# Work taken off GpSimd at the start, the epsilon in a 65th column, one factor moved to a later copy, 512 keys per score product, and an order worked out with other GpSimd durations

## The chip, the cores and the metric

One core of a Trainium2 chip runs the whole kernel. The metric is the device time of one execution in microseconds (us), lower is better. Five engines work side by side: TensorE (PE; its weight loads are a row of their own, PEld), VectorE (DVE), ScalarE (ACT), GpSimd (POOL) and SyncE (SP), which here only issues DMAs.

## The reference, cut to what matters

Two layers on 512 latent and 256 context tokens of width 1024, each of the form x + gate * mixer(adaLN(x)). In both, a token's input u goes through one large product into q, k, v and z, q and k are normalised per head, and the mixer's output is multiplied by silu(z) and goes through an output product.

```
e = silu(cvec) @ mod_w + mod_b                # shift, scale and gate of a layer
u = rms_norm(x, norm_g) * (1 + scale) + shift
q, k, v, z = split(u @ w_in, 4)
q = rms_norm(q, qn_g);  k = rms_norm(k, kn_g) # over 64 columns, eps 1e-6
# layer 0, differential attention, 16 heads (rope on latent q, k):
p = softmax(q k^T / 8);  o = (p[first] - lam * p[second]) @ v
y = rms_norm(o, subln_g) * (1 - lam_init) * silu(z)
# layer 1, neighbourhood attention, 32 heads: 8 x 16 window plus all context keys
o = softmax([q k_band^T / 8 + bias, q k_ctx^T / 8]) @ [v_band, v_ctx]
y = o * silu(z)
out = y @ w_out                               # then x + gate * out
```

## The kernel before

**Numbers.** Every large product is made in three products of rounded parts: a value is split into hi (a ScalarE copy to the rounded format) and lo (value minus hi, one subtraction), and hi*hi, hi*lo and lo*hi are added up in PSUM. The splits are most of the work of ACT and DVE: tiles `whi`/`wlo` for weights, `uhi`/`ulo` or `ufirst` for inputs, `mhl` for the weights of the first modulation, `wTa`/`wTb` for softmax weights.

**Stages.** Both layers work in 16 groups (two heads each). While a group's attention runs, the projection of the next group (`a_project`, `b_project`, PSUM tile `pj`) is laid between its steps. Ahead of layer 0's first group there is an opening: `mod_first` makes the modulation of layer 0 on PE (tile `pmod`, rows copied to `erow`, result in `mod0a`, `mod0b`), `norm_stats` makes the norm of each third of the tokens (`npart`, `nacc`, `nv`, `nr`, `ns`), `scaled` multiplies the input by it in place (`xin`), `first_u` applies the modulation (`ut`) and splits it (`ufirst`), and group 0 is projected as its inputs arrive. Between the layers lie the output product and the residual (`pjo`, `xres`).

**A projected tile** (`a_tile`, 96 times in layer 0; 80 alike in layer 1): `squares` on ACT (`sqk`), `rstd` sums them on DVE (`ssk`), scales and adds eps on POOL (`ssk` again), raises to -0.5 on POOL (`rsk`); `put_q` and `put_k` on DVE (`qd`, `kk`) then feed transposes on PE (`pq`, `pk`). `gate_z` makes z*(1+tanh) on DVE and, in layer 0, multiplies it on POOL by the sub-norm's gain (`Z`).

**After a group's attention in layer 0** (`a_norm`): PE transposes into `po`, ACT squares with a sum into `ms`, POOL adds eps*l^2 (`l0sq`) and raises to -0.5, DVE makes `y`, PE transposes it (`py`), ACT copies it out (`yT`) and it is stored.

**Layer 1's scores** (`b_scores`): for each of 16 groups, 2 heads and 4 query tiles, 256 band keys and 256 context keys, each a product with the hi and the lo part of q: four PE products of 256 columns.

**Order.** Nothing is issued as written. `Plan` records every instruction, estimates its duration (`estimate`), plays the run with a list scheduler (`order`: of the instructions ready on an engine the one recorded first) and issues them in the order played. Each engine then works through its fixed queue, so an instruction that is slower on the chip than in the play holds up what was placed right behind it. `LAG` and `AT` say at which step of a group things are recorded.

Of the kernel before, what the change touches and what calls it, by code (L numbers as in the profile page):

```python
# [10 lines left out]
F32 = mybir.dt.float32  # L11
# [18 lines left out]
def bc(ap, shape):  # L30
# [3 lines left out]
BUFS = dict(x8=2, wraw=2, whi=11, wlo=11, u=6, wT=4, qT=3, K=2, V=6, Z=5, ss=4, rs=4, nm=4,  # L34
            oT=1, y=1, yT=1, sq=1, t2=1, braw=1, tab=1, tab2=1)

# [5 lines left out]
FILL_A, FILL_B = (0, 1, 2, 3, 5, 7, 9, 11, 13, 15, 16, 17), (2, 4, 6, 8, 10, 11, 12, 13)  # L42
START_DVE = (0,)

# [6 lines left out]
NEXT = ((1, 2), (0, 1, 2), (1, 2), (0, 1, 2))  # L51
U_ACT = ((0, 0), (2, 0))
X_POOL, W_POOL, STAT_POOL = (2, 5, 6, 7, 9, 10, 11), (0, 1, 2, 3), ()
POOL_A, POOL_B = (), ()
# [29 lines left out]
class Op:  # L84
# [9 lines left out]
    def estimate(self, name):  # L94

        out, reads, e = self.writes[0], self.reads, self.engine
        n = math.prod(out.shape[1:])
        psum = any(x.space == PSUM for x in [out] + reads)
        if e == "PE":
            return 2.5 + n * (1 if reads[0].dtype == F32R else 2 if name == "transpose" else 4) / 2.4 if n > 2 else 260  # L100
        if e == "ACT":
            return n / 1.2 + (51 if psum else 93) + 93 * (len(self.writes) - 1 + name.startswith("act") * (len(reads) - 1))
        if e == "DVE":
            if name == "tensor_reduce":
                return math.prod(reads[0].shape[1:]) / 0.96 + 66
            if name in ("tensor_scalar", "tensor_copy", "memset") and not psum:
                return n / 1.92 + 69 + 60 * (len(reads) - 1)
            return n / 0.96 + (129 if len(reads) > 2 else 69)
        if e == "POOL":
            if any(x == ALU.pow for x in self.args):  # L110
                return 300 + 165 * n
            return n * 0.83 + 36 if name == "memset" else n * 2.1 + 150
        return max(56, math.prod(out.shape) / 90)
# [166 lines left out]
class K:  # L280
# [4 lines left out]
    def setup(self, es):  # L285
# [15 lines left out]
        self.mhalf = c.tile([P, 16], F32, name="mhalf")  # L301
        nc.vector.memset(self.mhalf, -0.5)

    def load_vecs(self):
# [128 lines left out]

    def norm_stats(self, x, tag="qd", on_pool=False):

# [4 lines left out]
        for kp in range(1, 4):  # L440
            sq = sb.tile([P, 2, 256], F32, name="sq", tag="pb")
            nc.scalar.activation(sq, x[kp], AF.Square)
            (nc.gpsimd if on_pool else nc.vector).tensor_tensor(part, part, sq, ALU.add)
        nc.vector.tensor_tensor(acc, part[:, 0], part[:, 1], ALU.add)
# [97 lines left out]
    def squares(self, x):  # L542
        sq = self.sb.tile([P, 2, P], F32, name="sqk", tag="sq")
        self.nc.scalar.activation(sq, x, AF.Square)
        return sq

    def rstd(self, sq):

        nc, sb = self.nc, self.sb
        ss = sb.tile([P, 4], F32, name="ssk", tag="ss")  # L550
        nc.vector.tensor_reduce(ss, sq.rearrange("p s (h d) -> p (s h) d", d=64), AX.X, ALU.add)
        nc.gpsimd.tensor_scalar(ss, ss, 1.0 / 64, EPS, ALU.mult, ALU.add)
        rs = sb.tile([P, 4], F32, name="rsk", tag="rs")
        nc.gpsimd.tensor_tensor(rs, ss, self.mhalf[:, 0:4], ALU.pow)
        return rs
# [40 lines left out]

    def gate_z(self, pz, dst, mul=None):
        nc = self.nc
        nc.vector.scalar_tensor_tensor(dst, dst, 1.0, pz, ALU.add, ALU.mult)
        if mul is not None:  # L600
            nc.gpsimd.tensor_tensor(dst, dst, mul, ALU.mult)

# [22 lines left out]
    def a_tables(self):  # L625
# [9 lines left out]
        for t in range(4):  # L635
            nc.vector.tensor_tensor(self.rc[:, t], self.rc[:, t], g[:, :, 0:64], ALU.mult)
            nc.vector.tensor_tensor(self.rs_[:, t], self.rs_[:, t], gs[:, :, 0:64], ALU.mult)
        tab2 = sb.tile([P, 2, P], F32, name="tab2", tag="tab2")
        self.gctx, self.subg = tab2[:, 0].rearrange("p (s d) -> p s d", s=2), tab2[:, 1]
        nc.vector.tensor_scalar(self.gctx[:, 0], g[:, 0, 0:64], 0.125, None, ALU.mult)  # L640
        nc.vector.tensor_copy(self.gctx[:, 1], g[:, 1, 0:64])

        nc.sync.dma_start(self.subg, A["subg"].broadcast_to([P, P]))
        nc.vector.tensor_scalar(self.subg, self.subg, 0.5 * (1.0 - LAM_INIT) * math.sqrt(P), None, ALU.mult)

        lv = sb.tile([P, 4, 64], F32, name="lv", tag="sq")
        nc.sync.dma_start(lv, A["lam"].unsqueeze(0).broadcast_to([P, 4, 64]))
# [13 lines left out]
    def a_tile(self, G, half, j, ps):  # L661
# [16 lines left out]
        nc.vector.tensor_tensor(V[:, 1, j], ps[:, 256:384], V[:, 0, j], ALU.subtract)  # L678
        self.gate_z(ps[:, 384:512], Z[:, j], mul=self.subg)
        qd = sb.tile([P, 2, 2, 64], F32, name="qd", tag="qd")  # L680
# [19 lines left out]
    def a_scores(self, g, G, half, j):  # L700
# [25 lines left out]
        nc.vector.scalar_tensor_tensor(sc, l[:, 0:1], self.nlam, r1, ALU.mult, ALU.mult)  # L726
        nc.gpsimd.tensor_tensor(l0sq[:, j : j + 1], l[:, 0:1], l[:, 0:1], ALU.mult)
        nc.vector.scalar_tensor_tensor(p[:, 0], p[:, 1], sc, p[:, 0], ALU.mult, ALU.add)
# [33 lines left out]
    def a_norm(self, g, G, half, oT, l0sq):  # L762
# [6 lines left out]
        for j in range(2):  # L769
            nc.scalar.activation(y[:, j], po[:, j], AF.Square, accum_out=ms[:, j : j + 1])  # L770
        nc.gpsimd.tensor_scalar(l0sq, l0sq, EPS * P, None, ALU.mult)
        nc.gpsimd.tensor_tensor(ms, ms, l0sq, ALU.add)
# [5 lines left out]
    def a_store(self, g, half, y):  # L778
        nc, sb = self.nc, self.sb
        py = self.pm.tile([P, 256], F32, name="py", tag="m")  # L780
        for j in range(2):
            nc.tensor.transpose(py[:, j * P : j * P + P], y[:, j], self.ident)
        if half < 2 and self.keep(0, g, py, slice(half * 256, half * 256 + 256)):
# [7 lines left out]
    def b_tables(self):  # L791
# [4 lines left out]
        self.gb = sb.tile([P, 2, 64], F32, name="gb", tag="tab2")  # L796
        nc.vector.tensor_scalar(self.gb[:, 0], g[:, 0, 0:64], -0.125, None, ALU.mult)
        nc.vector.tensor_copy(self.gb[:, 1], g[:, 1, 0:64])
        self.mask = sb.tile([P, 3, 256], F32, name="mask", tag="tab")
        nc.sync.dma_start(self.mask, A["mask"])  # L800
        self.pp = []
        for i in range(2):
            t = sb.tile([P, 2, 704], F32, name=f"pp{i}", tag="x8")
            nc.gpsimd.memset(t[:, :, 0:64], 0.0)
            nc.gpsimd.memset(t[:, :, 320:384], 0.0)
            self.pp += [t[:, 0], t[:, 1]]
# [62 lines left out]
    def b_bias(self, g, h):  # L869
# [5 lines left out]
        for geo in range(3):  # L875
            o = 128 - 64 * geo
            nc.vector.tensor_tensor(bm[:, geo], self.mask[:, geo], raw[:, o : o + 256], ALU.subtract)
        nc.gpsimd.memset(bm[:, 3], 0.0)
        self.bm[h] = bm

    def b_scores(self, g, G, h):
# [7 lines left out]
        for n in range(4):  # L889
# [10 lines left out]
            nc.vector.tensor_tensor_reduce(out=S2, in0=S2, in1=bm[:, geo : 4 : 3 - geo], op0=ALU.add, op1=ALU.min,  # L900
                                           scale=1.0, scalar=BIG, accum_out=nm)
            if n in (1, 2):
                p = self.pp[2 * h + n - 1]
                dst = p[:, 64:704].rearrange("p (a b) -> p a b", b=320)[:, :, 0:256]
            else:
# [8 lines left out]
    def b_weights(self, pn, kts):  # L914
# [3 lines left out]
        for kt in kts:  # L918
            ns = {0: (0, 1), 1: (0, 1, 2), 2: (1, 2, 3), 3: (2, 3)}.get(kt, (0, 1, 2, 3))
            pw = self.pm.tile([P, 512], F32, name="pwb", tag="m")  # L920
            for n in ns:
                if kt >= 4:
                    o = (384 if n in (1, 2) else 256) + (kt - 4) * P
                else:
                    o = (kt - (0, 0, 1, 2)[n]) * P
                nc.tensor.transpose(pw[:, n * P : n * P + P], pn[n][:, o : o + P], self.ident)
# [60 lines left out]

    def keep(self, layer, g, py, c):

        if g + 1 < NG:  # L990
            return False
        hi, lo = self.direct[layer]
        self.nc.scalar.copy(hi[:, c], py)
        self.nc.vector.tensor_tensor(lo[:, c], py, hi[:, c], ALU.subtract)
        self.kept += c.stop - c.start
# [83 lines left out]
    def run(self):  # L1079
# [12 lines left out]
        with ExitStack() as es:  # L1092
# [21 lines left out]
            with tc.tile_pool(name="ps0", bufs=3, space=PSUM) as ps0:  # L1114
# [3 lines left out]
                next(first)  # L1118
                r = self.norm_stats(xs[0], "Z", 0 in STAT_POOL)
                if SC0:  # L1120
# [11 lines left out]
                for n in range(4):  # L1132
                    for half in range(3):
                        if n == 0 and half:
                            self.scaled(xs[half], self.norm_stats(xs[half], "Z", half in STAT_POOL), half)
                        if half in NEXT[n]:
# [206 lines left out]
```

## Time and profile before

| | us |
|---|---|
| median of 3 runs | 1797.8 (1797.69 to 1799.71) |
| the profiled execution | 1795.94 |
| its span, first to last instruction | 1794.0 |
| PE busy | 1766.6 (98%) |
| PEld busy | 1506.1 (84%) |
| DVE busy | 1480.4 (83%) |
| ACT busy | 970.6 (54%) |
| POOL busy | 517.8 (29%) |

The profiled execution lasts 1.9 us longer than its span and is 1.9 us under the median. Products overlap on PE: a busy time is the time covered by at least one, so it also covers short stalls between two of them.

### The profile page before, as it was taken

Reading aid. Unit: us, or ns where it says so; the run is one execution under the profiler, and the core shown is the slowest. Engines: PE = TensorE matmul, PEld = TensorE weight load, DVE = VectorE, ACT = ScalarE, POOL = GpSimd, SP = SyncE. Lnnn points to the kernel's source line nnn. Section 1 sums busy time; section 2 is a strip of 40 time slices with the busy share of each in tenths; the row PEclk is TensorE's granted clock in tenths of the full one; section 3 lists DMA queues with packets and bytes.
Section 4 is the critical chain, followed back from the end, with each engine's and each line's share of the span. In section 5 each row is a group of like instructions: output and inputs, shape, how many; then the busy total and the mean of one; then the engine's idle time right before and its main releaser. Section 6 shows DMA issues by size and latency. Waiting matters only on the chain.

```text
span 1794.0 us, 29417 instructions
## 1 busy us (share of the span) xinstructions
PE 1766.6 (98%) x10032; PEld 1506.1 (84%) x10032; DVE 1480.4 (83%) x3493; ACT 970.6 (54%) x2654; POOL 517.8 (29%) x859
## 2 busy tenths in 40 slices
PE   7899999999999999999999999999999999999999
PEld 3688888888888888888888988888888888888887
DVE  5889999889999999989867777778878877787863
ACT  4455555555555555555645545555555555555641
POOL 4544344344444434344200021121112111222100
PEclk9999999999999999999999999999999999999999
DMA  7401222212222222223547411212222222112423
GB/s 286 140 16 57 77 69 63 69 54 69 80 77 80 66 80 75 70 92 100 172 126 241 159 52 63 62 63 67 65 73 73 63 74 74 63 62 74 146 89 105
DMA packets 60773, 160.73 MB, mean 90 GB/s; under 512 B 7376, under 2 KB 22096, under 8 KB 59728
## 3 DMA queue, kind: packets, MB, share of 16 engines
q1 hardware_dynamic: 60624, 158.86, 27.3%
q8 instruction: 79, 1.29, 0.3%
q14 instruction: 70, 0.57, 0.1%
HBM read 144.68 MB, written 14.16 MB: 89 GB/s over the span
## 4 chain that ended last, share of the span: by engine, by line
PE 85%; DVE 7%; ACT 4%; POOL 2%; issue 1%; DMA 1%; SPq 0%; DVEq 0%; ACTq 0%
PE pj L277 46%; PE pjo L277 12%; PE S L277 5%; PE oT L277 4%; PE oTb L277 4%; PE pwb L277 4%; PE Sb L277 3%; ACT pexp L277 2%; PE pq L277 2%; POOL ms L277 2%; PE pw L277 2%; PE pk L277 1%; DVE nm L277 1%; DVE y L277 1%; PE py L277 1%
## 5 line engine op out<-in xcount | busy, mean ns | idle before, releaser
L277 PE MATMUL pj<-whi,ufirst 128*128 128x512 f32 x1536 | 523.9, 401 | 2.4 <-ACT ufirst L277 1.9
L277 PEld LDWEIGHTS pj<-whi,ufirst 128*128 128x128 f32 x1536 | 289.5, 189 | 57.9 <-ACT ufirst L277 2.5
L277 PE MATMUL pj<-wlo,ufirst 128*128 128x512 f32 x768 | 302.9, 394 | 0.0
L277 PE MATMUL pj<-whi,uhi 128*128 128x512 f32 (+1 forms) x768 | 279.3, 364 | 0.0
L277 PE MATMUL pj<-whi,ulo 128*128 128x512 f32 (+1 forms) x768 | 276.5, 360 | 0.0
L277 PE MATMUL pj<-wlo,uhi 128*128 128x512 f32 (+1 forms) x768 | 276.0, 360 | 0.0
L277 ACT CAST whi<-wraw 128x512 fp32r<-128x512 f32 x352 | 208.7, 629 | 97.2 <-PE pjo L277 32.6
L277 DVE TENSOR_TENSOR wlo<-wraw,whi 128x512 fp32r<-128x512 f32 x344 | 230.5, 696 | 31.6 <-ACT whi L277 30.7
L277 ACT ACTIVATE pexp<-S,nm 128x768 f32<-128x768 f32 (+1 forms) x192 | 144.0, 757 | 127.9 <-DVE nm L277 127.8
L277 POOL TENSOR_SCALAR ssk<-ssk 128x4 f32<-128x4 f32 x176 | 35.1, 199 | 610.2 <-DVE ssk L277 608.2
L277 PE MATMUL pjo<-yhl,whi 128*128 128x512 f32 (+1 forms) x768 | 208.0, 357 | 0.0
L277 POOL TENSOR_TENSOR rsk<-ssk,mhalf 128x4 f32<-128x4 f32 x176 | 179.4, 1019 | 14.5
L277 PEld LDWEIGHTS pj<-wlo,ufirst 128*128 128x128 f32 x768 | 145.4, 189 | 26.4
L277 PEld LDWEIGHTS pj<-whi,ulo 128*128 128x128 f32 x768 | 145.1, 189 | 18.9
L277 PEld LDWEIGHTS pj<-wlo,uhi 128*128 128x128 f32 x768 | 145.2, 189 | 16.6
L277 PEld LDWEIGHTS pj<-whi,uhi 128*128 128x128 f32 x768 | 145.2, 189 | 16.2
L277 PEld LDWEIGHTS pjo<-yhl,whi 128*128 128x128 f32 x768 | 134.8, 189 | 18.3
L277 DVE TENSOR_REDUCE nm<-S 128x2 f32<-128x1536 f32 (+1 forms) x96 | 133.9, 1395 | 6.2 <-PE S L277 6.1
L277 PE MATMUL pjo<-yhl,wlo 128*128 128x512 f32 (+1 forms) x384 | 136.7, 356 | 0.0
L277 ACT ACTIVATE sqk<-pj 128x256 f32<-128x256 f32 x176 | 67.5, 384 | 124.3 <-PE pj L277 119.8
L277 PE MATMUL S<-KS,qT 128*128 128x256 f32 (+1 forms) x640 | 132.8, 336 | 0.0
L277 ACT CAST wTb<-pwb 128x512 fp32r<-128x512 f32 (+2 forms) x192 | 87.1, 488 | 70.0 <-PE pwb L277 69.5
(161 smaller groups left out, 3483.6 us busy)
## 6 DMA issues: line engine op xcount, KB each, us to landing
wraw<-wa SPq DMA_DIRECT2D x64, 512.0 KB, 3.5
wraw<-wb SPq DMA_DIRECT2D x64, 512.0 KB, 3.6
modw<-modw SPq DMA_DIRECT2D x48, 512.0 KB, 3.7
wraw<-wo SPq DMA_DIRECT2D x24, 512.0 KB, 3.9
wraw<-wo SPq DMA_DIRECT2D x48, 256.0 KB, 3.2
yraw<-yd SPq DMA_DIRECT2D x14, 512.0 KB, 3.8
braw<-rpb SPq DMA_DIRECT2D x32, 192.0 KB, 2.4
yd<-yT SPq DMA_DIRECT2D x30, 128.0 KB, 1.9
```

Source lines behind the costliest of these rows:

```text
L277: op.f(*op.args, **op.kw)
```

## The change

1. In the opening, no subtraction or product runs on POOL any more: 12 of the 16 `mhl` subtractions (`START_DVE`), 7 of the 12 `xin` products (`X_POOL`) and the 8 `wlo` subtractions of group 0 (`W_POOL`) go to DVE. Four `ut` (half 1, even k) go from DVE to ACT (`U_ACT`). The powers (`nr`) stay on POOL.
2. `squares` writes into one constant tile with 65 columns per head, the last of which holds 64*eps; the sum then has eps in it, and the POOL instruction that scaled and added it goes (176 times). The factor 8 that is left over moves into the tables of gains.
3. The sub-norm's gain is no longer multiplied into `Z` (96 POOL products); it is the scale of the copy from `py` (`yT`, and `keep` for the last group).
4. eps*128 is multiplied in where l^2 is made, so that 48 POOL instructions of `a_norm` go.
5. `b_scores` reads context and band keys with one access pattern: two products of 512 columns in place of four of 256. Keys stand in the order context, band, and `bm` and the padded tiles `pp` follow.
6. `estimate` has other durations for POOL, so the order played is another one.

```diff
-START_DVE = (0,)
+START_DVE = (0, 1, 2, 3)
-U_ACT = ((0, 0), (2, 0))
-X_POOL, W_POOL, STAT_POOL = (2, 5, 6, 7, 9, 10, 11), (0, 1, 2, 3), ()
+U_ACT = ((0, 0), (1, 0), (2, 0))
+X_POOL, W_POOL = (), ()
...
             if any(x == ALU.pow for x in self.args):
-                return 300 + 165 * n
-            return n * 0.83 + 36 if name == "memset" else n * 2.1 + 150
+                return 402 + 153 * n
+            if n <= 4:
+                return 957 if name == "tensor_tensor" and n == 2 else 400 if n == 1 else 210
+            return n * 0.83 + 36 if name == "memset" else n * 2.35 + 110
...
+        self.sq = c.tile([P, 4, 65], F32, name="sqk")
+        nc.vector.memset(self.sq[:, :, 64:65], 64 * EPS)
...
     def squares(self, x):
-        sq = self.sb.tile([P, 2, P], F32, name="sqk", tag="sq")
-        self.nc.scalar.activation(sq, x, AF.Square)
-        return sq
+        self.nc.scalar.activation(self.sq[:, :, 0:64], x.rearrange("p s (h d) -> p s h d", d=64), AF.Square)
+        return self.sq
...
-        nc.vector.tensor_reduce(ss, sq.rearrange("p s (h d) -> p (s h) d", d=64), AX.X, ALU.add)
-        nc.gpsimd.tensor_scalar(ss, ss, 1.0 / 64, EPS, ALU.mult, ALU.add)
+        nc.vector.tensor_reduce(ss, sq, AX.X, ALU.add)
...
-    def gate_z(self, pz, dst, mul=None):
+    def gate_z(self, pz, dst):
-        if mul is not None:
-            nc.gpsimd.tensor_tensor(dst, dst, mul, ALU.mult)
...
-        nc.gpsimd.tensor_tensor(l0sq[:, j : j + 1], l[:, 0:1], l[:, 0:1], ALU.mult)
+        nc.gpsimd.tensor_scalar(l0sq[:, j : j + 1], l[:, 0:1], l[:, 0:1], EPS * P, ALU.mult, ALU.mult)
...
-        nc.gpsimd.tensor_scalar(l0sq, l0sq, EPS * P, None, ALU.mult)
...
-        nc.scalar.copy(yT, py)
+        nc.scalar.activation(yT, py, AF.Copy, scale=self.subg)
...
-            for c, k in ((0, k0), (256, 0)):
-                for i in range(2):
-                    nc.tensor.matmul(S[:, c : c + 256], qT[:, i, h, (n % 2) * P : (n % 2) * P + P],
-                                     KS[:, h, k : k + 256], start=(i == 0), stop=(i == 1))
+            k = KS[:, h, 0:512].rearrange("p (a b) -> p a b", a=2)
+            k = type(k)(k.tensor, k.offset, (k.ap[0], (k0, 2), (1, 256)))
+            for i in range(2):
+                nc.tensor.matmul(S, qT[:, i, h, (n % 2) * P : (n % 2) * P + P], k, start=(i == 0), stop=(i == 1))
```

## Rows read from the trace of the kernel before

**Rows 1.** Windows: stretch, length, busy us of PE, PEld, DVE, ACT, POOL; PEclk, DMA.

```profile
0.00:92.00 92.00, 72.55 (x335) 47.27 (x336) 66.60 (x130) 43.62 (x91) 47.08 (x47) 0.94 0.59 208
...
160.00:860.00 700.00, 696.84 (x3823) 587.76 (x3822) 641.34 (x1532) 395.25 (x1223) 290.60 (x497) 1.00 0.23 74
...
1060.00:1700.00 640.00, 640.00 (x3881) 561.87 (x3881) 514.55 (x1272) 356.51 (x923) 124.07 (x210) 1.00 0.23 72
```

**Rows 2.** Waits of PE over the span: us in total, times, longest us.

```profile
PE pmod L277 <- DMA modw<-modw: 9.0, 1, 9.0
PE pmod L277 <- DVE erow L277: 7.5, 4, 3.2
PE pj L277 <- ACT ufirst L277: 1.9, 2, 1.7
PE py L277 <- DVE y L277: 1.3, 6, 0.4
```

**Rows 3.** Timeline of DVE in the opening: start, us for the run of instructions.

```profile
32.77 2.50 DVE L277 TENSOR_SCALAR ut<-xin,mod0a,mod0b 128x256 f32<-128x256 f32 x2
...
73.44 1.05 DVE L277 TENSOR_SCALAR ut<-xin,mod0a,mod0b 128x256 f32<-128x256 f32 x3
...
76.45 1.29 DVE L277 TENSOR_TENSOR wlo<-wraw,whi 128x512 fp32r<-128x512 f32 x2
```

**Rows 4.** Timeline of POOL in the opening.

```profile
32.08 4.31 POOL L277 TENSOR_TENSOR xin<-xin,ns 128x512 f32<-128x512 f32 x3
```

**Rows 5.** Groups of DVE in the stretch 20:85, shapes apart: count, busy us, mean ns.

```profile
L277 DVE TENSOR_SCALAR ut<-xin,mod0a,mod0b 128x256 f32<-128x256 f32 x16 | 12.0, 793 | 0.1
...
L277 DVE TENSOR_TENSOR xin<-xin,ns 128x512 f32<-128x512 f32 x4 | 5.3, 1346 | 4.3 <-ACT ns L277 4.3
...
L277 DVE TENSOR_TENSOR mhl<-modw,mhl 128x512 fp32r<-128x512 f32 x3 | 4.2, 1404 | 0.0
...
L277 DVE TENSOR_TENSOR nacc<-npart 128x256 f32<-128x256 f32 x2 | 2.8, 1414 | 0.0
```

**Rows 6.** Groups of POOL over the span, shapes apart.

```profile
L277 POOL TENSOR_TENSOR Z<-Z,tab 128x128 f32<-128x128 f32 x96 | 54.5, 568 | 0.2
...
L277 POOL TENSOR_SCALAR ssk<-ssk 128x4 f32<-128x4 f32 x176 | 35.1, 199 | 610.2 <-DVE ssk L277 608.2
...
L277 POOL TENSOR_TENSOR mhl<-modw,mhl 128x512 fp32r<-128x512 f32 x12 | 17.2, 1448 | 18.8 <-ACT mhl L277 18.8
```

**Rows 7.** Windows of the opening, columns as in the first group.

```profile
26.00:30.00 4.00, 4.00 (x14) 2.74 (x14) 2.94 (x5) 1.95 (x4) 1.66 (x1) 0.57 1.03 410
```

**Rows 8.** Timeline of PE in layer 1.

```profile
1199.73 0.39 PE L277 MATMUL pj<-wlo,uhi 128*128 128x512 f32 x1
...
1202.68 0.39 PE L277 MATMUL pj<-whi,ulo 128*128 128x512 f32 x1
...
1203.92 1.68 PE L277 MATMUL Sb<-KSb,qT 128*128 128x256 f32 x12
1205.43 0.40 PE L277 MATMUL pj<-whi,uhi 128*128 128x512 f32 x1
...
1208.18 0.64 PE L277 MATMUL Sb<-KSb,qT 128*128 128x256 f32 x4
1208.66 0.60 PE L277 MATMUL pq<-ident,qd 128*128 128x128 f32 x4
```

**Rows 9.** Waits of PE's weight loads over the span.

```profile
PEld py L277 <- DVE y L277: 13.5, 41, 0.7
...
PEld pq L277 <- DVE qd L277: 6.9, 14, 0.7
```

**Rows 10.** Chain that ended last in the stretch 330:352: start, us, what.

```profile
329.34 0.97 POOL ms L277
...
330.38 0.72 POOL ms L277
...
331.12 0.62 DVE y L277 x2
```

More of the change, by code (lines that the diff above doesn't have):

```diff
@@ L34 @@
 BUFS = dict(x8=2, wraw=2, whi=11, wlo=11, u=6, wT=4, qT=3, K=2, V=6, Z=5, ss=4, rs=4, nm=4,
-            oT=1, y=1, yT=1, sq=1, t2=1, braw=1, tab=1, tab2=1)
+            oT=1, y=1, yT=1, t2=1, braw=1, tab=1, tab2=1)
 LAG = dict(pw=2.5, pv=1.5, po=0.5, py=1.5, qka=2, qkb=3, b1=2, b2=1.5, b3=1, bo=0.5, by=3)
@@ L51 @@
 NEXT = ((1, 2), (0, 1, 2), (1, 2), (0, 1, 2))
-U_ACT = ((0, 0), (2, 0))
-X_POOL, W_POOL, STAT_POOL = (2, 5, 6, 7, 9, 10, 11), (0, 1, 2, 3), ()
+U_ACT = ((0, 0), (1, 0), (2, 0))
+X_POOL, W_POOL = (), ()
+SQ_PE = (False, False, False)
 POOL_A, POOL_B = (), ()
@@ L431, in mod_finish, with norm_stats @@
         return r
-    def norm_stats(self, x, tag="qd", on_pool=False):
+    def norm_stats(self, x, tag="qd", on_pe=False):
         nc, sb = self.nc, self.sb
@@ L442, in norm_stats @@
             nc.scalar.activation(sq, x[kp], AF.Square)
-            (nc.gpsimd if on_pool else nc.vector).tensor_tensor(part, part, sq, ALU.add)
+            nc.vector.tensor_tensor(part, part, sq, ALU.add)
         nc.vector.tensor_tensor(acc, part[:, 0], part[:, 1], ALU.add)
@@ L595, in k_transposed @@
         nc.vector.tensor_tensor(KS[0:64, 1, s], pk[64:128], KS[64:128, 1, s], ALU.subtract)
-    def gate_z(self, pz, dst, mul=None):
-        nc = self.nc
-        nc.vector.scalar_tensor_tensor(dst, dst, 1.0, pz, ALU.add, ALU.mult)
-        if mul is not None:
-            nc.gpsimd.tensor_tensor(dst, dst, mul, ALU.mult)
+    def gate_z(self, pz, dst):
+        self.nc.vector.scalar_tensor_tensor(dst, dst, 1.0, pz, ALU.add, ALU.mult)
     def gained(self, out, x, g):
@@ L635, in a_tables @@
         for t in range(4):
[L636 to L643, printed above, removed]
+            nc.vector.scalar_tensor_tensor(self.rc[:, t], self.rc[:, t], 8.0, g[:, :, 0:64], ALU.mult, ALU.mult)
+            nc.vector.scalar_tensor_tensor(self.rs_[:, t], self.rs_[:, t], 8.0, gs[:, :, 0:64], ALU.mult, ALU.mult)
+        tab2 = sb.tile([P, P], F32, name="tab2", tag="tab2")
+        self.gctx = tab2.rearrange("p (s d) -> p s d", s=2)
+        self.subg = c.tile([P, 1], F32, name="subg")
+        nc.vector.tensor_copy(self.gctx[:, 0], g[:, 0, 0:64])
+        nc.vector.tensor_scalar(self.gctx[:, 1], g[:, 1, 0:64], 8.0, None, ALU.mult)
+        nc.sync.dma_start(self.subg, A["subg"].rearrange("a p -> p a"))
         nc.vector.tensor_scalar(self.subg, self.subg, 0.5 * (1.0 - LAM_INIT) * math.sqrt(P), None, ALU.mult)
-        lv = sb.tile([P, 4, 64], F32, name="lv", tag="sq")
+        lv = sb.tile([P, 4, 64], F32, name="lv", tag="qd")
         nc.sync.dma_start(lv, A["lam"].unsqueeze(0).broadcast_to([P, 4, 64]))
@@ L678, in a_tile @@
         nc.vector.tensor_tensor(V[:, 1, j], ps[:, 256:384], V[:, 0, j], ALU.subtract)
-        self.gate_z(ps[:, 384:512], Z[:, j], mul=self.subg)
+        self.gate_z(ps[:, 384:512], Z[:, j])
         qd = sb.tile([P, 2, 2, 64], F32, name="qd", tag="qd")
@@ L782, in a_store @@
             nc.tensor.transpose(py[:, j * P : j * P + P], y[:, j], self.ident)
-        if half < 2 and self.keep(0, g, py, slice(half * 256, half * 256 + 256)):
+        if half < 2 and self.keep(0, g, py, slice(half * 256, half * 256 + 256), self.subg):
             return
         yT = sb.tile([P, 256], F32, name="yT", tag="yT")
-        nc.scalar.copy(yT, py)
+        nc.scalar.activation(yT, py, AF.Copy, scale=self.subg)
         y = self.yd[0][g // 2, :, g % 2, half] if half < 2 else self.ye[g // 2, :, g % 2, 0]
@@ L796, in b_tables @@
         self.gb = sb.tile([P, 2, 64], F32, name="gb", tag="tab2")
-        nc.vector.tensor_scalar(self.gb[:, 0], g[:, 0, 0:64], -0.125, None, ALU.mult)
-        nc.vector.tensor_copy(self.gb[:, 1], g[:, 1, 0:64])
+        nc.vector.tensor_scalar(self.gb[:, 0], g[:, 0, 0:64], -1.0, None, ALU.mult)
+        nc.vector.tensor_scalar(self.gb[:, 1], g[:, 1, 0:64], 8.0, None, ALU.mult)
         self.mask = sb.tile([P, 3, 256], F32, name="mask", tag="tab")
@@ L802, in b_tables @@
         for i in range(2):
-            t = sb.tile([P, 2, 704], F32, name=f"pp{i}", tag="x8")
-            nc.gpsimd.memset(t[:, :, 0:64], 0.0)
-            nc.gpsimd.memset(t[:, :, 320:384], 0.0)
+            t = sb.tile([P, 2, 640], F32, name=f"pp{i}", tag="x8")
+            nc.gpsimd.memset(t[:, :, 256:320], 0.0)
+            nc.gpsimd.memset(t[:, :, 576:640], 0.0)
             self.pp += [t[:, 0], t[:, 1]]
@@ L876, in b_bias @@
             o = 128 - 64 * geo
-            nc.vector.tensor_tensor(bm[:, geo], self.mask[:, geo], raw[:, o : o + 256], ALU.subtract)
-        nc.gpsimd.memset(bm[:, 3], 0.0)
+            nc.vector.tensor_tensor(bm[:, geo + 1], self.mask[:, geo], raw[:, o : o + 256], ALU.subtract)
+        nc.gpsimd.memset(bm[:, 0], 0.0)
         self.bm[h] = bm
@@ L893, in b_scores @@
             qT = G["q"][1 + n // 2]
-            for c, k in ((0, k0), (256, 0)):
-                for i in range(2):
-                    nc.tensor.matmul(S[:, c : c + 256], qT[:, i, h, (n % 2) * P : (n % 2) * P + P],
-                                     KS[:, h, k : k + 256], start=(i == 0), stop=(i == 1))
+            k = KS[:, h, 0:512].rearrange("p (a b) -> p a b", a=2)
+            k = type(k)(k.tensor, k.offset, (k.ap[0], (k0, 2), (1, 256)))
+            for i in range(2):
+                nc.tensor.matmul(S, qT[:, i, h, (n % 2) * P : (n % 2) * P + P], k, start=(i == 0), stop=(i == 1))
             S2 = S.rearrange("p (a b) -> p a b", a=2)
             nm = sb.tile([P, 1], F32, name="nmb", tag="nm")
-            nc.vector.tensor_tensor_reduce(out=S2, in0=S2, in1=bm[:, geo : 4 : 3 - geo], op0=ALU.add, op1=ALU.min,
+            nc.vector.tensor_tensor_reduce(out=S2, in0=S2, in1=bm[:, 0 : geo + 2 : geo + 1], op0=ALU.add, op1=ALU.min,
                                            scale=1.0, scalar=BIG, accum_out=nm)
@@ L903, in b_scores @@
                 p = self.pp[2 * h + n - 1]
-                dst = p[:, 64:704].rearrange("p (a b) -> p a b", b=320)[:, :, 0:256]
+                dst = p.rearrange("p (a b) -> p a b", b=320)[:, :, 0:256]
             else:
@@ L921, in b_weights @@
             for n in ns:
[L922 to L925, printed above, removed]
+                o = (kt - 4) * P if kt >= 4 else 256 + (kt - (0, 0, 1, 2)[n]) * P
                 nc.tensor.transpose(pw[:, n * P : n * P + P], pn[n][:, o : o + P], self.ident)
@@ L985, in b_store, with keep @@
         nc.sync.dma_start(self.yd[1][g // 2, :, g % 2], yT)
-    def keep(self, layer, g, py, c):
+    def keep(self, layer, g, py, c, gain=None):
         if g + 1 < NG:
@@ L992, in keep @@
         hi, lo = self.direct[layer]
-        self.nc.scalar.copy(hi[:, c], py)
-        self.nc.vector.tensor_tensor(lo[:, c], py, hi[:, c], ALU.subtract)
+        if gain is None:
+            self.nc.scalar.copy(hi[:, c], py)
+            self.nc.vector.tensor_tensor(lo[:, c], py, hi[:, c], ALU.subtract)
+        else:
+            self.nc.scalar.activation(hi[:, c], py, AF.Copy, scale=gain)
+            self.nc.vector.scalar_tensor_tensor(lo[:, c], py, gain, hi[:, c], ALU.mult, ALU.subtract)
         self.kept += c.stop - c.start
@@ L1118, in run @@
                 next(first)
-                r = self.norm_stats(xs[0], "Z", 0 in STAT_POOL)
+                r = self.norm_stats(xs[0], "Z", SQ_PE[0])
                 if SC0:
@@ L1134, in run @@
                         if n == 0 and half:
-                            self.scaled(xs[half], self.norm_stats(xs[half], "Z", half in STAT_POOL), half)
+                            self.scaled(xs[half], self.norm_stats(xs[half], "Z", SQ_PE[half]), half)
                         if half in NEXT[n]:
```

## The prediction

> **What bounds the kernel now.** I read the windows by stage first. From 160 us on PE is covered almost without a gap: 696.84 of 700 us in layer 0, 640.00 of 640 in layer 1 [rows 1]. The other engines have slack there, DVE least (641 of 700). So behind the opening only three things can shorten the run: less work on PE, fewer short stalls that the busy time hides, or an earlier start. The opening differs: in the first 92 us PE is busy 72.55 us at a mean clock of 0.94 [rows 1].
>
> Next the waits of PE. The first product waits 9.0 us for its weights from DMA, which the change doesn't touch. Then come waits for DVE: 7.5 us for `erow` in four waits, and 1.9 us for `ufirst`, released by ACT, which itself had waited for DVE's `ut` [rows 2]. Together 9.4 us.
>
> Why DVE is late there is seen in its timeline. Two `ut` products begin at 32.77 and take 2.50 us; later three of them take 1.05 us, 0.35 each [rows 3]. POOL was running three `xin` products from 32.08 to 36.39 in the first case [rows 4]. The group means show the same: in 20:85 a `ut` takes 793 ns against 350, a 512-column `xin` or `mhl` 1346 or 1404 ns against 645 (two `wlo` in 1.29 us, [rows 3]), a `nacc` 1414 ns for 256 columns, which at half of 645 should take some 320 [rows 5]. I read it as DVE standing still while POOL works. The stretch is 16 x 0.443 + 4 x 0.701 + 3 x 0.759 + 2 x 1.09 = 7.1 + 2.8 + 2.3 + 2.2 = 14.4 us.
>
> The clock adds a second loss. In 26:30 it was granted at 0.57, so most of the stretch ran at the lower level of 1.2 GHz [rows 7]; that is one of three such stretches of 4 us, all in the opening and each behind a gap in PE's work. They lose 3 x 4 x 0.43 = 5.2 us.
>
> Last the waits of weight loads, since a stall shorter than a product's drain doesn't show as PE idle: `py` waits 13.5 us for `y` in 41 waits, `pq` 6.9 us for `qd` in 14 [rows 9], while PE itself counts only 1.3 us for `py` [rows 2].
>
> **The change part by part.** The sum is made against the profiled execution, 1795.94 us (span 1794.0 and 1.9 around it), which lies 1.9 us under the median of 1797.8.
>
> *Opening.* 12 + 7 + 8 = 27 instructions go from POOL to DVE, which has 27 x 0.645 = 17.4 us more; four `ut` leave it, 4 x 0.35 = 1.4. Net +16.0. If the stretch of 14.4 us goes, since only the short powers are left on POOL, DVE has 1.6 us more than before: 68 of 92 us. As a load that is no gain. As lateness it is one: POOL took 1448 ns for what DVE does in 645 [rows 6], so each split is ready sooner, and the stretched instructions stood right ahead of `erow` and `ufirst`. Most gained is 9.4 + 5.2 = 14.6 us (all waits and all of the clock's loss), least nothing, if the new DVE work falls ahead of the same results. With DVE about as loaded as before I take 4 us of the waits, a little under half, and 2 of the clock's 5.2: 6 us. An earlier start moves everything behind it, as PE has no gap to absorb it; what is late next is the weights of group 1, already split on DVE.
>
> *Scores of layer 1.* 16 x 2 x 4 = 128 score tiles each lose two of four products. Four of 256 columns take from 1208.18 to 1208.66, 0.48 us. Products of 512 columns follow each other in (1202.68 - 1199.73) / 13 = 0.227 us, two in 0.454 [rows 8]. Saved: 0.026 x 128 = 3.3 us. Another run gives more: twelve from 1203.92 to 1205.43, 0.126 each, four in 0.503 [rows 8], so 0.05 x 128 = 6.3; but its first product follows transposes. No row shows a product whose moving operand is read in two pieces, so the lower end is nothing. I take 3.3, by the run that stands between two products of its own kind on PE's path. All of it counts, as PE has no gap in 1060:1700.
>
> A page speaks against this part. The Trainium skill, "TensorE: Matmul & The Clock Gate", section "Back-to-back issue gap", gives 2.5 ns beside the columns per isolated product at the full clock, so that two products fewer would save 5 ns a tile, an estimate of 0.6 us for 128, and the sum would be 2.7 us worse. The same formula gives about 109 ns for 256 columns, where this trace has 120 and 126, and 216 for 512, where it has 227.
>
> *Stalls in layer 0, through the order.* A chain that ended at `py` shows POOL at `ms` for 0.97 and 0.72 us and DVE at `y` for 0.62 [rows 10]. The play of before has 154 + 96 + 630 = 880 ns for the two POOL steps (150 + 2.1 x 2, the gap between two POOL instructions, 300 + 165 x 2), so `py` is placed some 0.8 us too early. The new figures give 957 + 96 + 708 = 1761 ns, against the 1.69 of the rows. With the right figure another ready product goes ahead of `py`, and PE loses nothing by it. The same holds for `qd`: `ssk` on POOL (0.199 us, [rows 6]) leaves its chain. What PE loses at `py` and `pq` lies between the 1.3 us of [rows 2] and 13.5 + 6.9 = 20.4 us of [rows 9]. I take half, 10, and expect 4 of them back, since other waits will be misplayed and a new order can make its own. Bounds: 10 gained, or 4 lost.
>
> *At nothing.* POOL's `Z` products (54.5 us), `ssk` (35.1) and 48 `l0sq` leave an engine that is busy 291 of 700 us [rows 1, 6]; beyond the chain above nobody waits for them. The 65th column makes the sum 260 columns instead of 256. The one constant `sqk` tile serialises squares and sums as the single buffer did. The scaled copy of `py` (46 copies, and two in `keep`) may be longer, at most by the 0.568 us of the POOL product that it replaces [rows 6], 27 us of ACT in a stage where ACT is idle 305 us [rows 1]; behind it in ACT's queue stand splits for DVE, so without that slack it would cost a part of those 27. In `keep` DVE has one more operand, twice. The DMA of the sub-norm's gain keeps its place in SP's queue with 128 values, and its first reader is now the first copy of `py`. No wait is added on POOL or SP.
>
> Sum: 6 + 3.3 + 4 = 13.3. From 1795.94 that is 1782.6, and 1784.5 on the scale of the median.
>
> **The rivals.**
> - *The opening is freed wholly.* For it: all PE waits after the first are behind stretched DVE instructions. Against it: DVE's load is no smaller. 14.6 + 3.3 + 8 (twice my share of the stalls) = 25.9, so 1772.
> - *The opening gains nothing*: 16.0 us of new work on DVE takes up what the stretch frees, and `erow` is late behind splits instead. 3.3 + 4: 1790.5.
> - *Products in two pieces cost as much as the four did*, or two products of 512 save only what the page's formula says. For it: no row has such an operand. 6 + 4: 1787.8; the estimate by the page (0.6) lies beside it.
> - *The change doesn't do what it says*: the order matters as much as the durations, a new one brings as many stalls as it takes, and only the scores are left, 1794.5, or nothing at all, 1797.8.
> - *Slower: DVE becomes the bound of the opening.* The stretch is not POOL's doing, or the powers left on POOL cause it as well; then DVE has 16.0 us more in front of the first group's results. With 3.3 + 4 gained later that is 8.7 us slower, 1806.5. It decides from 10.9 us lost in the opening on. Against it speaks that three `ut` took 1.05 us with POOL idle [rows 3], and that DVE was idle 25 of 92 us [rows 1].
>
> **How the numbers follow.** A difference under 0.2% (3.6 us) can't be told from none here. Chances: forecast 0.42, opening freed 0.13, opening without gain 0.17, scores without gain 0.09, no effect 0.11, slower 0.08. Faster: 0.42 + 0.13 + 0.17 + 0.09 = 0.81; same 0.11; slower 0.08. The range reaches from the freed opening, 1772, to the scores alone, 1795; the likeliest case's own is 1778 to 1790 (opening 2 to 12, scores and stalls as taken).
>
> **What would show it.** In the profile after: `ut` in the opening near 350 ns and 512-column products near 650 on DVE; PE's waits for `erow` and `ufirst` well under 9.4 us, and fewer stretches at the lower clock; the first group's projection done some 6 us sooner; `Sb` in 256 products, two in about 0.454 us; weight loads waiting less than 20.4 us at `py` and `pq`. The forecast is wrong if `erow` waits as long behind DVE's splits, if a product read in two pieces takes more than 0.24 us, or if the new order opens gaps in PE behind 160 us, where there were 3.2 in layer 0.

## The result, and the profile after

The changed kernel takes 1770.1 us (median, 1769.5 to 1771.7) against 1797.7: a ratio of 0.985 (0.983 to 0.986), 27.6 us less. The prediction was 1784.5 with a range down to 1772: the time lies 1.9 us below the range, the sign was right, and the size was half of what came. The profiled execution has a span of 1768.2 us against 1794.0, 25.8 less.

Windows of the kernel after, columns as in [rows 1]:

```profile
0.00:92.00 92.00, 75.90 (x371) 51.48 (x372) 69.21 (x178) 48.83 (x102) 13.75 (x18) 0.98 0.58 207
...
160.00:860.00 700.00, 700.00 (x3901) 600.24 (x3900) 643.65 (x1564) 409.07 (x1251) 234.21 (x303) 1.00 0.25 80
```

In the opening PE is busy 3.4 us longer and its clock is at 0.98 of full speed instead of 0.94 [rows 1]; it falls in one stretch, from 44 to 52 us, instead of three. In layer 0 the telling figure is not the busy time, which was nearly full before, but the count: 3901 products in the same 700 us, where there were 3823, so that one product takes 0.179 us on average instead of 0.183.

Waits of PE, columns as in [rows 2]:

```profile
PE ss L280 <- POOL nr L280: 2.6, 2, 1.6
PE pmod L280 <- DVE erow L280: 1.5, 1, 1.5
PE pj L280 <- ACT ufirst L280: 0.9, 2, 0.5
PE pj L280 <- DVE ufirst L280: 0.8, 1, 0.8
```

The waits for `erow` and `ufirst` are down from 9.8 us (the 9.4 of [rows 2], and 0.4 for `ufirst` behind DVE) to 3.2; a new one, 2.6 us for the power `nr` on POOL, has come (below). DVE's groups in 20:85, to be read against [rows 5]:

```profile
L280 DVE TENSOR_TENSOR mhl<-modw,mhl 128x512 fp32r<-128x512 f32 x12 | 7.9, 678 | 0.7 <-ACT mhl L280 0.7
L280 DVE TENSOR_TENSOR xin<-xin,ns 128x512 f32<-128x512 f32 x11 | 6.9, 683 | 2.2 <-ACT ns L280 2.2
L280 DVE TENSOR_SCALAR ut<-xin,mod0a,mod0b 128x256 f32<-128x256 f32 x12 | 4.5, 401 | 0.0
```

DVE does four times as many `mhl` and nearly three times as many `xin`, each in half the time, and a `ut` takes 401 ns instead of 793.

The chain that ended last in 330:352 (the stretch of [rows 10]), shares by line:

```profile
by line: PE pj L280 67.9%; PE oT L280 14.2%; PE pw L280 6.9%; PE S L280 5.9%; PE po L280 2.0%; PE pq L280 2.0%; PE py L280 1.0%; PE pk L280 1.0%
```

It runs through PE alone. Before, POOL's `ms` and DVE's `y` were links of it. Of the weight loads' waits, 13.5 us at `py` and 6.9 at `pq` for `qd` [rows 9], this is left; for `qd` there is none:

```profile
PEld py L280 <- DVE y L280: 0.4, 1, 0.4
```

The scores, in PE's timeline (compare [rows 8]):

```profile
1181.89 1.63 PE L280 MATMUL Sb<-KSb,qT 128*128 128x512 f32 x6
1183.35 0.40 PE L280 MATMUL pj<-whi,uhi 128*128 128x512 f32 x1
...
1186.09 0.63 PE L280 MATMUL Sb<-KSb,qT 128*128 128x512 f32 x2
1186.56 0.60 PE L280 MATMUL pq<-ident,qd 128*128 128x128 f32 x4
```

Two products take 0.47 us where four took 0.48; six take 1.46 where twelve took 1.51.

By the traces of the two kernels, the gain of 25.8 us falls like this. The first product of layer 0's scores (`S`) begins at 90.5 us instead of 97.3: the opening is 6.8 shorter. From there to the first product of `pjo` it takes 757.6 us instead of 772.1, 14.5 less, and from the first to the last `Sb` of layer 1 635.0 instead of 639.8, 4.8 less. Between the layers 0.3 us are lost.

### The profile page after: what moved, and what is told of

The parts are those of the page before. It is cut to its first block, busy times and chain, and to the rows that moved or that the text cites. A ratio compares the mean times of both kernels' runs of the same rounds, so it can differ in the third digit from the quotient of the medians.

```text
span 1768.2 us, 28647 instructions
## 1 busy us (share of the span) xinstructions
PE 1748.2 (99%) x9776; PEld 1493.1 (84%) x9776; DVE 1465.5 (83%) x3517; ACT 977.5 (55%) x2658; POOL 395.6 (22%) x512
## 4 chain that ended last, share of the span: by engine, by line
PE 97%; DVE 2%; ACT 0%; DMA 0%; issue 0%; POOL 0%; SPq 0%; DVEq 0%; ACTq 0%
PE pj L280 54%; PE pjo L280 13%; PE S L280 6%; PE oT L280 5%; PE oTb L280 4%; PE pwb L280 4%; PE Sb L280 3%; PE pw L280 3%; PE pq L280 2%; PE pk L280 1%; PE pmod L280 1%; PE py L280 1%; PE po L280 1%; PE pyb L280 0%; PE pob L280 0%; DVE xin L280 0%
## 5 line engine op out<-in xcount | busy, mean ns | idle before, releaser
L280 PEld LDWEIGHTS pj<-wlo,ufirst 128*128 128x128 f32 x768 | 145.3, 189 | 25.8
L280 PE MATMUL S<-KS,qT 128*128 128x256 f32 (+1 forms) x640 | 125.8, 331 | 0.2 <-DVE Z L280 0.2
L280 DVE TENSOR_TENSOR wTb<-pwb,wTb 128x512 fp32r<-128x512 f32 (+2 forms) x192 | 99.4, 552 | 24.0 <-ACT wTb L280 23.2
```

Of the source, the lines that this page charges most:

```text
L280: op.f(*op.args, **op.kw)
```

## The experiments

The theory: DVE stands still while GpSimd works, which costs the opening 7 to 10 us; and the order is played with a GpSimd step that is too short, which costs layer 0 more than I had counted. The rivals: GpSimd is merely a slow producer, or the stalls of layer 0 go because GpSimd instructions are gone from the chains. Every time stands beside runs of the kernel before on the same chip, at 1797.2 to 1799.1 us.

**Each part alone, and the durations taken back.** `b_est`: the kernel before with the new `estimate`. (In the edits, `...` marks lines left out.)

```diff
-                return 300 + 165 * n
-            return n * 0.83 + 36 if name == "memset" else n * 2.1 + 150
+                return 402 + 153 * n
+            if n <= 4:
+                return 957 if name == "tensor_tensor" and n == 2 else 400 if n == 1 else 210
+            return n * 0.83 + 36 if name == "memset" else n * 2.35 + 110
```

> The kernel before with the new GpSimd durations in the estimate alone, so the same instructions in another order. The order theory (the misplayed chain to py and qd is what stalls PE in layer 0) expects the weight loads' waits at py and pq to fall from 13.5 + 6.9 us to under 5, layer 0 (between the opening and the output product) to be 8 to 12 us shorter, and the opening as slow as before: 1785 to 1791. The trimming theory (the stalls go because the GpSimd instructions are gone from the chains) expects less than 3 us from it: 1795 to 1799.

1785.0 us, 12.7 less (ratio 0.993, 0.9915 to 0.9942). The wait at `py` is gone and at `pq` 3.1 us are left, while PE in the opening waits nearly as before (8.9 us for `erow` and `ufirst`). In its trace the first `S` comes no sooner, at 97.7, and the stretch from there to `pjo` is 12.9 us shorter, with 3897 products in 160:860. The same instructions in another order give nearly half of the whole gain.

`b_open`: the kernel before with the opening's constants.

```diff
-START_DVE = (0,)
+START_DVE = (0, 1, 2, 3)
-U_ACT = ((0, 0), (2, 0))
+U_ACT = ((0, 0), (1, 0), (2, 0))
-X_POOL, W_POOL, STAT_POOL = (2, 5, 6, 7, 9, 10, 11), (0, 1, 2, 3), ()
+X_POOL, W_POOL, STAT_POOL = (), (), ()
```

> The kernel before with the opening's products and subtractions on DVE alone (three lines of constants). The port theory (DVE stands still while GpSimd works) expects 7 to 10 us less in the first 92 us and the stalls of layer 0 as before, 1787 to 1791. If the opening owes its gain to the new durations in the play, it is under 3 us: 1795 to 1799.

1788.8 us, 9.0 less (0.995, 0.9936 to 0.9964). Its window and its weight loads' waits:

```profile
0.00:92.00 92.00, 76.98 (x372) 51.24 (x373) 69.77 (x178) 48.74 (x103) 15.56 (x30) 0.98 0.59 208
```

```profile
PEld py L277 <- DVE y L277: 13.5, 42, 0.6
...
PEld pq L277 <- DVE qd L277: 7.1, 15, 0.7
```

The opening is close to that of the changed kernel (the first `S` begins at 88.6), the stalls of layer 0 are those of before, with 3826 products in 160:860: the two gains are separate. The edit also moves four `ut` to ACT; their share of the 9.0 is not shown.

`b_scores`: the kernel before with the two products of 512 columns, the order of keys and the tiles `bm` and `pp` that go with it.

```diff
-            for c, k in ((0, k0), (256, 0)):
-                for i in range(2):
-                    nc.tensor.matmul(S[:, c : c + 256], qT[:, i, h, (n % 2) * P : (n % 2) * P + P],
-                                     KS[:, h, k : k + 256], start=(i == 0), stop=(i == 1))
+            k = KS[:, h, 0:512].rearrange("p (a b) -> p a b", a=2)
+            k = type(k)(k.tensor, k.offset, (k.ap[0], (k0, 2), (1, 256)))
+            for i in range(2):
+                nc.tensor.matmul(S, qT[:, i, h, (n % 2) * P : (n % 2) * P + P], k, start=(i == 0), stop=(i == 1))
...
```

> The kernel before with the two products of 512 columns per score tile alone. The prediction's term expects 3.3 us less, 1794.5. By the profile after, two products in two pieces take about as long as four did (0.47 to 0.49 us), which gives 1 to 1.5 us: 1796.5.

1794.9 us, 2.8 less (0.998, 0.9975 to 0.9992, so 1.4 to 4.5 us). The interval holds 3.3; it leaves out 1.3 us or less. In the trace the stretch from the first to the last `Sb` is 3.2 us shorter (636.6 against 639.8).

`a_noest`: the changed kernel with the old figures.

```diff
-                return 402 + 153 * n
-            if n <= 4:
-                return 957 if name == "tensor_tensor" and n == 2 else 400 if n == 1 else 210
-            return n * 0.83 + 36 if name == "memset" else n * 2.35 + 110
+                return 300 + 165 * n
+            return n * 0.83 + 36 if name == "memset" else n * 2.1 + 150
```

> The changed kernel with the old GpSimd durations in the estimate. The order theory expects py to wait again, though with a chain that is shorter by two instructions: 6 to 12 us more than the changed kernel, 1776 to 1782. The trimming theory expects under 3 us more, 1770 to 1773.

1775.7 us (0.988, 0.9861 to 0.9891), 5.6 more than the changed kernel, just under the expected stretch; weight loads wait 8.2 us at `py` again. With the trimmed instructions gone the old figures cost less than half of what they cost before, so the trimming repairs a part of the same stalls.

**Which figure it is.** `b_ms`: one figure in the kernel before.

```diff
+            if n == 2 and name == "tensor_tensor":
+                return 957
             return n * 0.83 + 36 if name == "memset" else n * 2.1 + 150
```

> The kernel before with one figure of the estimate alone: 957 ns for a GpSimd sum of two columns (the step ms + l0sq), where it had 154. The order theory puts most of the gain of the new durations on this one step of the chain to py: the weight loads' wait at py falls from 13.5 to under 2 us, that at pq stays near 6.9, and the kernel gains 7 to 10 us: 1788 to 1791. If the gain came from the play being different at all, or from the other figures, it is under 4 us: 1794 to 1798.

1784.8 us (0.993, 0.9913 to 0.9946): the whole 12.4 us, more than I had expected. The weight loads' waits:

```profile
PEld pq L279 <- DVE qd L279: 2.9, 14, 0.3
...
PEld py L279 <- DVE y L279: 0.3, 1, 0.3
```

The wait at `py` is gone, and that at `pq` has fallen by more than half although no duration in its own chain was changed: it is still 14 waits, but shorter ones. Why `pq` gains too is not shown.

`a_ms154`: the changed kernel without that figure.

```diff
-                return 957 if name == "tensor_tensor" and n == 2 else 400 if n == 1 else 210
+                return 154 if name == "tensor_tensor" and n == 2 else 400 if n == 1 else 210
```

> The changed kernel with the one figure of ms + l0sq put back from 957 to 154 ns in the estimate. The order theory expects what all old durations together did (1775.7): py waits about 8 us in its weight loads and the kernel takes 1774 to 1777. If the other figures matter as well, it stays at 1770 to 1773.

1776.5 us (0.988, 0.9862 to 0.9895), 5 to 6.4 us more than the changed kernel (the kernel before was 1.3 us slower on that chip), and 8.1 us in the waits at `py`. The one figure does what all of them did.

`a_long`: the changed kernel with the figure too large.

```diff
-                return 957 if name == "tensor_tensor" and n == 2 else 400 if n == 1 else 210
+                return 2500 if name == "tensor_tensor" and n == 2 else 400 if n == 1 else 210
```

> The changed kernel with 2500 ns in place of 957 for the step ms + l0sq in the estimate, so that py is played 1.5 us later than it can be. The order theory says that only a play that is too early costs anything: other products fill the time and the kernel is within 2 us of the changed one, 1769 to 1772. If the play has to be right both ways, it is over 4 us slower: 1774 to 1780.

1770.9 us (0.985, 0.9837 to 0.9866), the changed kernel's time. A play that is 1.5 us too late costs nothing that can be measured; one that is 0.8 us too early costs this kernel 5 to 6.4 us (`a_ms154`), and it cost the kernel before 12.4 (`b_ms`).

**The trimmed instructions.** `b_trim`: the kernel before with the changes to `squares`, `rstd`, `gate_z`, `a_scores`, `a_norm`, `a_store`, `keep` and their tables alone.

```diff
...
-        nc.gpsimd.tensor_scalar(ss, ss, 1.0 / 64, EPS, ALU.mult, ALU.add)
...
-            nc.gpsimd.tensor_tensor(dst, dst, mul, ALU.mult)
...
-        nc.gpsimd.tensor_scalar(l0sq, l0sq, EPS * P, None, ALU.mult)
...
```

> The kernel before with the eps column, the gain at the copy of py and the eps with l squared, the opening, the scores and the old durations as they were: 320 GpSimd instructions fewer. With the old durations the changed kernel without them cost 5.6 us, and the opening and the scores are worth 9.0 and 2.8, so 27.6 - 5.6 - 9.0 - 2.8 = 10 us should be this part's when the durations are old: 1787 to 1789, with the wait at py down to about 8 us and that at pq gone. If the trimmed instructions were off the path as the prediction said, it gains under 3 us: 1795 to 1798.

1790.1 us, 7.0 less (0.995, 0.9939 to 0.9969): less than expected by difference, but not nothing. The wait at `py` falls to 7.9 us, and that at `pq` for `qd` to 0.2.

`b_trim_est`: the same with the new `estimate` (the diff of `b_est`).

> The kernel before with the trimmed instructions and the new durations, opening and scores as before. Alone the trimming gave 7.0 us and the durations 12.7. If both repair the same stalls, together they give little over 12.7, and what the trimming adds is the 3.1 us that are left of 27.6 after opening, durations and scores: 1781 to 1783. If they are separate, 19 to 20 us: 1777 to 1779.

1783.6 us, 13.6 less (0.992, 0.9904 to 0.9937), 0.9 more than `b_est` alone gave, and the 3.1 us that `b_est` left at `pq` are gone. The two repair in the main the same stalls.

`b_open_est`: the diffs of `b_open` and `b_est` together.

> The kernel before with the opening on DVE and the new durations, without the trimmed instructions and the new scores. If the two add up, 9.0 + 12.7 = 21.7 us less: 1775 to 1777. If they overlap in the opening (the durations also order it), less than 19: 1779 or more.

1775.9 us, 21.3 less (0.988, 0.9862 to 0.9892): opening and durations add up.

**What GpSimd does to the opening.** `a_dead`: the changed kernel with 27 subtractions and products more on GpSimd, whose results nobody reads.

```diff
-X_POOL, W_POOL = (), ()
+X_POOL, W_POOL = (), (0, 1, 2, 3)
...
+                        if m % 4:
+                            nc.gpsimd.tensor_tensor(self.junk.rearrange("p (a b) -> p a b", a=2), lo, hi, ALU.subtract)
...
+            if 4 * half + n in (2, 5, 6, 7, 9, 10, 11):
+                self.nc.gpsimd.tensor_tensor(self.junk.rearrange("p (a b) -> p a b", a=2), x[n],
+                                             s.unsqueeze(1).broadcast_to([P, 2, 256]), ALU.mult)
...
+            if eng:
+                eng.tensor_tensor(self.junk, lo, hi, ALU.subtract)
```

> The changed kernel, in whose opening GpSimd makes the 27 subtractions and products as well, right behind DVE's, into a scratch tile that nobody reads; DVE's are the ones that count, so no result comes from GpSimd later than before. The port theory (DVE stands still while GpSimd works) expects DVE's ut and 512-column instructions in the opening to be stretched again, by 10 us or more in all, and the kernel to be 6 to 12 us slower than the changed one: 1776 to 1782. The late-producer theory (before, the splits came late because GpSimd takes twice as long for one) expects no stretch that matters: 1770 to 1772.

1792.5 us (0.997, 0.9959 to 0.9982): 22 us more than the changed kernel, far over what the port theory had expected. The GpSimd instructions added here also read tiles of the opening and so can hold their buffers, which the next run takes away.

`a_dead2`: the same number of dead products in the same places, on a tile of their own; each is released by a column (`flag`) that ACT copies from DVE's result.

```diff
...
+                            self.dead(lo[:, 0, 0:1])
...
+    def dead(self, x):
+        f = self.flag[:, self.flags : self.flags + 1]
+        self.flags += 1
+        self.nc.scalar.copy(f, x)
+        self.nc.gpsimd.tensor_tensor(self.junk, self.junk, f.broadcast_to([P, 512]), ALU.mult)
...
```

> The changed kernel with 27 dead GpSimd products in the opening as in the run before it (1792.5), but on a scratch tile and a flag that ACT copies from one column of DVE's result, so that GpSimd reads no tile of the opening and holds no buffer. If the stretch of DVE made all of the 22 us, this is 1788 to 1793, with ut at 0.8 to 1.0 us again. If held buffers made the part beyond the 9 us of the opening alone, it is 1777 to 1783. If GpSimd costs DVE nothing, 1770 to 1773 (27 short copies on ACT are added).

1787.3 us (0.994, 0.9922 to 0.9952): 16 to 17 us more than the changed kernel, a little under the stretch of the first case and well over the second. Its groups of POOL and, in 20:85, of DVE:

```profile
L280 POOL TENSOR_TENSOR junk<-junk,flag 128x512 f32<-128x512 f32 x27 | 36.3, 1344 | 29.1 <-ACT flag L280 27.6
```

```profile
L280 DVE TENSOR_TENSOR ufirst<-ut,ufirst 128x512 fp32r<-128x512 f32 x11 | 11.2, 1039 | 1.2 <-ACT ufirst L280 1.2
L280 DVE TENSOR_SCALAR ut<-xin,mod0a,mod0b 128x256 f32<-128x256 f32 x12 | 10.5, 905 | 0.0
L280 DVE TENSOR_TENSOR mhl<-modw,mhl 128x512 fp32r<-128x512 f32 x12 | 9.8, 836 | 0.0
```

A `ut` takes 905 ns against 401, with GpSimd on a tile that DVE touches only once, to fill it; the three groups together take some 12 us more than at the changed kernel's durations. All of the time is lost in the opening: the first `S` begins at 108.2 us instead of 90.5, and layer 0 is as long as in the changed kernel. PE waits 12.1 us for `erow` and `ufirst` there instead of 3.2, and its clock is granted at 0.87 in the first 92 us instead of 0.98, so the time lost holds a share of the clock as well. The late producer has fallen as the main cause: nothing waits for the dead products, and for the powers `nr`, the one result that GpSimd still makes for the opening, PE waits 1.0 us (2.6 in the changed kernel).

Two things are not separated. The copies of the flag make ACT wait 9.3 us for DVE; that this starves DVE is unlikely, since for its splits and `xin` DVE waits 2.7 us for ACT in the opening where it waits 11.0 in the changed kernel. And the 5 us between the two runs fit the held buffers, but the order differs as well, so that share is not shown.

**The scores again, and a version that is faster still.** `a_noscores`: the changed kernel with the old scores (the diff of `b_scores` reversed).

> The changed kernel with four products of 256 columns per score tile again. By the spacing in the profiles (two of 512 in two pieces 0.47 to 0.49 us, four of 256 in 0.48 to 0.50) it is 1 to 1.5 us slower than the changed kernel: 1771 to 1772. By the prediction's term 3.3 us: 1773.4. The part alone, in the kernel before, gave 2.8 us.

1773.6 us (0.986, 0.9844 to 0.9874), 3.5 more than the changed kernel's first runs; the kernel before was 1.3 us slower on that chip, so 2 to 3.5. From the first to the last `Sb` it takes 638.8 us against 635.0, 3.8 more.

`a_erow`: the copies of the modulation's rows on ACT.

```diff
-                nc.vector.tensor_copy(row, ps)
+                nc.scalar.copy(row, ps)
```

> The changed kernel with the 8 copies to erow on ACT instead of DVE, so that PE's modulation no longer queues behind DVE's splits. If DVE's queue is what PE waits for in the opening, PE's wait for erow (1.5 us) goes and the kernel takes 1767 to 1769.5. If the opening hangs on the inputs' norm and on DMA instead, nothing changes: 1769.5 to 1771.

1767.8 us (0.983, 0.9814 to 0.9843). Then once more, beside the changed kernel on one chip:

> The changed kernel itself, beside the next one on the same chip: 1769.5 to 1772.

> The changed kernel with the 8 copies to erow on ACT once more, beside the changed kernel: 2 to 4 us under it if the first run's 1767.8 holds, within 1 us if that was the spread of runs.

1770.3 and 1767.8 us. Against the kernel before on that chip the ratios are 0.985 (0.9831 to 0.9861) and 0.983 (0.9817 to 0.9847), whose intervals overlap; but every run of the copies on ACT, 1767.1 to 1768.8 in both series, lies under every run of the changed kernel beside it, 1769.7 to 1771.2. The copies on ACT save 2.5 us: PE's wait for `erow` falls from 1.5 to 0.5 us, though that for `ufirst` by way of ACT rises from 0.9 to 2.1.

## Why the prediction was too small

**The step that failed is the third term**, the stalls in layer 0: "I take half, 10, and expect 4 of them back, since other waits will be misplayed and a new order can make its own". Measured alone it is 12.7 us (`b_est`), 8.7 more than the term. Both discounts were wrong. The weight loads' waits at `py` and `pq` fell by 20.4 - 3.1 = 17.3 us and the time by 12.7, so PE lost about 0.7 of such a wait, not half (in `b_trim` 7.0 of 12.3, nearer to it). And nearly all came back: the new order left hardly a wait in layer 0, where PE is busy in all of the 700 us. The mechanism was as written: `py` was played 0.8 us too early because of one step, 154 ns in the play against 0.97 in the chain [rows 10], and that figure alone gives 12.4 us. (What the prediction did not know is why the step takes so long: it is held up by DVE, see the last section.) That a play which errs to the late side is free here (`a_long`) is what the term needed; I had treated it as a gamble on a new order.

**The opening** was taken at 6 and measured at 9.0 (`b_open`), inside its bounds of 0 and 14.6. The ledger was nearly right: DVE ended 3.2 us busier than before, 69.8 us against 66.6 [rows 1], where it had 1.6. The shares were low on both sides: the waits for `erow` and `ufirst` fell from 9.8 to 4.7 us in that run, 5.1 where I took 4, and the clock rose from 0.94 to 0.98 over 92 us, 3.7 us where I took 2. In the changed kernel's own trace the opening is 6.8 us shorter, so there the 6 was nearly met, and the layers hold more of the gain.

**The scores** were taken at 3.3 and measured at 2.8 and 2 to 3.5; the term holds, and so does the length of the stage in the traces, 3.2 and 3.8 us. On PE's own timeline less is to be seen: 0.01 us for each pair that stands alone and 0.05 / 3 for each of three in a row, some 2 us for 128. A product in two pieces follows the last in 0.235 us in a pair and in 0.243 in a row of six, just over the 0.24 that the prediction had named as a sign against it, so the rival of the two pieces was partly right. The Trainium skill's formula ("TensorE: Matmul & The Clock Gate", "Back-to-back issue gap"), with the estimate of 0.6 us worked out from it, falls short of the 2.8 and lies outside the interval.

**At nothing** stood the trimmed POOL instructions. Beside the right durations that holds within the noise (0.9 us, `b_trim_est` against `b_est`); without them they are worth 7.0 us. The wait at `pq` goes, as the prediction had written of `ssk`; why that at `py` falls to 7.9 as well is not shown, a shorter queue on POOL being the likely reason.

**The rest.** Opening, durations and scores are 9.0 + 12.7 + 2.8 = 24.5 of 27.6 us. What remains is 3.1; the trimming shows 0.9 of it, and the last 2 us are within what the separate medians leave uncertain. The likeliest case's own range has a slip: an opening of 2 us with scores and stalls as taken gives 1788.5, not 1790. It changes nothing here.

**The rivals.** "The opening is freed wholly" came nearest in time, 1772, for another reason: the opening gave 9 of its 14.6 us, the stalls more than its 8. "Slower" was wrong: the stretch goes with GpSimd's work, and comes back with it in `a_dead2`.

## What to carry to other kernels

Where an order is played from estimated durations, measure each small step of a long chain, and measure it in its place, with the other engines at work: alone the step here takes about what the old figure said, 0.2 us, and in its place mostly 0.84 to 0.96. That one figure cost more here (12.4 us) than 320 instructions (7.0), and too long a figure cost nothing. Look at the waits of the weight loads and at products per stretch, since PE's busy time hid three quarters of this loss (3.2 us of idle time in layer 0 [rows 1] for 12.7 lost). Before work is shared between DVE and GpSimd, compare DVE's own durations with GpSimd busy and idle: a product given to GpSimd was paid for on DVE.

## What the runs showed of the hardware that was not expected

GpSimd is held up by DVE, and not only the other way round. In the changed kernel one power of two columns, 0.70 us at best, takes 2.88 us. The timelines of POOL and DVE:

```profile
37.63 2.88 POOL L280 TENSOR_TENSOR nr<-nv,mhalf 128x2 f32<-128x2 f32 x1 [9.33 <-DVE nv L280]
```

```profile
37.47 1.89 DVE L280 TENSOR_TENSOR mhl<-modw,mhl 128x512 fp32r<-128x512 f32 x3
39.27 0.69 DVE L280 TENSOR_TENSOR wlo<-wraw,whi 128x512 fp32r<-128x512 f32 x1
```

It ends at 40.51, some 0.55 us after four subtractions in a row on DVE have ended at 39.96; that is the new wait of PE for `nr`. In `a_erow` the same power begins in the same row of subtractions, ends 0.56 us after the first of them and takes 1.07 us; in `a_erow_b`, the same kernel once more, it takes 2.88 again. These two executions last 1768.06 and 1768.08 us, so the longer power cost nothing that can be measured there.

The step whose figure cost 12.4 us is held up in the same way. In the kernel before, the sum of `ms` and `l0sq` that opens the chain of [rows 10], beside the DVE instruction that runs when it begins:

```profile
329.34 0.96 POOL L277 TENSOR_TENSOR ms<-ms,l0sq 128x2 f32<-128x2 f32 x1 [0.91 <-ACT y L277]
```

```profile
329.23 1.02 DVE L277 SCALAR_TENSOR_TENSOR pexp<-pexp,sc 128x768 f32<-128x768 f32 x1
```

DVE's ends at 330.25, the sum 0.05 us later. Of the 48 sums of that kernel 39 take 0.38 to 0.96 us, and every one of them ends 0.04 to 0.06 us after the DVE instruction that was running when it began; that instruction always reads two inputs from SBUF (`pexp`, `mjunk`, `wlo` or `qd`). The other nine take 0.19 to 0.20: beside a short instruction on one column, beside none, or beside a `wTa`, one of whose inputs lies in PSUM. So the old figure of 154 ns was about right for the step alone, and the new 957 is in the main a wait for DVE.

The Trainium skill, "SBUF — State Buffer", section "SBUF: two separate sides", says that the two engines share a pair of ports as an exclusive lock, held for a whole instruction, which the engine that starts first gets; DVE contends for it with instructions in a two-port mode, or with two inputs in SBUF against a GpSimd instruction that reads SBUF. The sums, these rows and `a_dead2` agree with it, in both directions; why the power sometimes waits for one instruction of DVE's row and sometimes for all four, no run here shows.
